# Eight down projections in seven products, six pairs of k's each, where six had four pairs

## The chip, the cores and the metric

The kernel runs on one core of one Trainium2 chip. The metric is the device time of one execution in microseconds (us). The kernel before took 2079.3 us (median of three runs, 2079.28 to 2080.11).

## The reference

Two layers over 256 tokens of width 2048, all in float32. The first layer mixes with a state space model and a gated recurrence, the second with windowed attention; after each comes the same MLP, whose up projection is 2048 to 8192 and whose down projection is 8192 to 2048. What the change touches is the down projection and what reads its result: the norm ahead of attention after the first MLP, and the output after the second.

```python
def squared_relu_mlp(xn, w_up, w_down):
    return jnp.square(jax.nn.relu(xn @ w_up)) @ w_down

def reference(...):
    h = x
    for layer in range(DEPTH):
        ...
        h = h + y.astype(h.dtype)
        h = h + squared_relu_mlp(rms_norm(h, mlp_norm[layer]), mlp_w_up[layer], mlp_w_down[layer])
    return h
```

## The kernel before

**Three matmuls for a product.** Each float32 operand is split into a high part in the matmul's own format and the rest (`hi`, `lo`), and a product is three matmuls: hi by hi, hi by lo, lo by hi. A weight is loaded as a unit of 1024 columns of 128 partitions (512 KB): `emit_dma` (L98) issues the load from SP into a buffer `raw`, `emit_split` (L131) lets ScalarE write `hi` (L141) and VectorE write `lo = raw - hi` (L142), and TensorE uses both (all matmuls are recorded at L190). `advance` (L145) hands the units out in one fixed order, a list called `units`. Loads go ahead through eight buffers: four of a pool (`raw`), and four more for odd units of an MLP (they are a part of the tile `chi`); a buffer takes its next load once the split of what it holds is done. Split weights have four buffers, and two more for every fourth unit.

**The MLP** (`mlp`, L984) works in four chunks c of 2048 hidden columns. `up(c)` makes the chunk's activations `ch[c]` (16 k's of 128 rows, 256 tokens in two halves t), `down(c)` multiplies them by 2048 rows of `w_down` and adds four blocks n of 512 columns to `h`. The plain way takes 8 products for a pair of k's, two halves t and two blocks n. `down_mixed` (L1038) takes 7 for the blocks 0 and 1, by sums and differences of the four quarters of an activation pair (`forms`, made in `up`, L1025 to L1032) and of the weights (`combine`, L117, on VectorE at L120). One pair j needs four units with names of their own: `t1` (two products), `t42` (two products, after two subtractions of 512 and 1024 columns that need t1's raw weights), later `b2` (two products) and `b12` (one product; its load is 256 KB, and its subtraction needs b2's raw weights). t1 has a subtraction of 512 columns, b12 too, b2 none. A product is accumulated in one of four banks `a_`, `c_`, `e_`, `f_`; after the last t42 ScalarE copies three of them, and after the last b12 VectorE forms the results (L1076 to L1081). The two blocks n = 2 and 3 stay plain: a plain unit is two k's by 512 columns and takes 12 matmuls of 512 columns, a unit t1, t42 or b2 takes 6, a b12 takes 3. `down_plan` (L310 to L321) is the order of the units of a chunk: four pairs (NS = 4) with plain units between them, then the pairs 4 to 7 of the blocks 0 and 1 as plain units. Below, a unit is named by kind and pair (t42.3), a plain one by block and pair (p3.1).

**The last chunk** (c = 3) is plain in all four blocks: `down` calls `xblock` for n = 0 to 3, adds each block to `h` and hands it to `nxt.block(n)`. That is `Norm.block` (L951) after the first MLP: squares on ScalarE, transposes on TensorE (L386) and two writes of the next operand `XT`; or `Out.block` (L964) after the second: two stores.

**The order.** A scheduler places the instructions on each engine's queue when the kernel is built, by the order of the program and its own idea of durations. Each engine then runs its queue in that order. So VectorE, standing at a combination whose load has not landed, does nothing else, though splits of older units are behind it.

Of the kernel before, what the change touches and what calls it, by code (L numbers as in the profile page):

```python
# [9 lines left out]
F32R = mybir.dt.float32r  # L10
# [7 lines left out]
P = 128  # L18
# [42 lines left out]
def hybrid_kernel(ctx: ExitStack, tc: tile.TileContext, x, even_norm, even_w_in, s5_lambda_re, s5_lambda_im,  # L61
# [208 lines left out]
    w_qkv, w_out1 = odd_w_qkv[0], odd_w_out[0]  # L270
    K16, K8 = list(range(16)), list(range(8))
    S5C, HC = 1024, 512
    in_cols = [0, 512]
# [13 lines left out]
    def add_mlp(l):  # L287
        def up(c):
            for n in range(8):
                add_units(mlp_w_up[l], K16, c * 2048 + n * 256, 256)  # L290

        def down(c):
            if c == 3:
                for n in range(4):
                    add_units(mlp_w_down[l], [c * 16 + k for k in K16], n * 512)
                return
            for kind, n, i in down_plan:
                if kind is None:
                    add_units(mlp_w_down[l], [c * 16 + 2 * i, c * 16 + 2 * i + 1], n * 512)
                else:  # L300
                    units.append((mlp_w_down[l], c * 16 + 2 * i + (kind in ("t42", "b2")),
                                  512 if kind == "b12" else 0, 2, kind))

        for c in range(4):
            up(c)
            down(c)
        ends.append(len(units))


    NS = 4  # L310
    plain = [(None, n, i) for n in (2, 3) for i in range(8)]
    down_plan = []
    for j in range(NS):
        down_plan += [("t1", 0, j), plain.pop(0), ("t42", 0, j), plain.pop(0)]
        if j < 2:
            down_plan.append(plain.pop(0))
    for j in range(NS):
        down_plan += [("b2", 0, j), plain.pop(0), ("b12", 0, j)]
        if plain and j < 2:
            down_plan.append(plain.pop(0))  # L320
    down_plan += plain + [(None, n, i) for n in (0, 1) for i in range(NS, 8)]  # L321

    add_mlp(0)
    qkv_cols = [2048, 0, 512, 1024, 1536]
    for c in qkv_cols:
        add_units(w_qkv, K16, c)
    out1_passes = [list(range(0, 8)), list(range(8, 12)), list(range(12, 16))]
# [616 lines left out]
    class Norm:  # L944
        def __init__(self, gain):
            self.gain, self.XT = gain, new_pair("x")
            self.ss = cp.tile([P, 2, 4], F32, name="ss" + gain)
            self.rs = cp.tile([P, 2], F32, name="rs" + gain)
            self.rs2 = cp.tile([P, 2], F32, name="rs2" + gain)

        def block(self, n):  # L951
            for t in range(2):
                j = t4([P, 512])
                S.activation(out=j, in_=h[:, t, n * 512:(n + 1) * 512], func=AF.Square,
                             accum_out=self.ss[:, t, n:n + 1])
            make_xT(h, self.XT, self.gain, 4 * n, 4)
            if n == 3:
                V.tensor_reduce(out=self.rs, in_=self.ss, axis=AX.X, op=ALU.add)
                V.tensor_scalar(out=self.rs, in0=self.rs, scalar1=1.0 / D, scalar2=EPS, op0=ALU.mult, op1=ALU.add)
                V.reciprocal(out=self.rs2, in_=self.rs)  # L960
                G.tensor_tensor(out=self.rs, in0=self.rs, in1=nhalf.to_broadcast([P, 2]), op=ALU.pow)
# [22 lines left out]
    def mlp(norm, nxt):  # L984
# [22 lines left out]
        def up(c):  # L1007
            ch[c] = new_pair("c")
            if c < 3:
                forms[c] = sp.tile([P, 2, NS, 4, P], F32R, tag="q1", name="forms", bufs=1)  # L1010
            for n in range(8):
# [11 lines left out]
                                op=ALU.subtract)  # L1023
                if c < 3 and n < NS:
                    a11, a21, a12, a22 = [r[:, k, t * P:(t + 1) * P] for k in range(2) for t in range(2)]  # L1025
                    s_ = t4([P, 4, P])
                    for o, a, b, op in ((0, a21, a22, ALU.add), (1, a11, s_[:, 0], ALU.subtract),
                                        (2, a11, a21, ALU.subtract), (3, a12, s_[:, 1], ALU.add)):
                        V.tensor_tensor(out=s_[:, o], in0=a, in1=b, op=op)
                    fh, fl = forms[c][:, 0, n], forms[c][:, 1, n]  # L1030
                    S.copy(out=fh, in_=s_)
# [6 lines left out]
        def down_mixed(c):  # L1038
# [15 lines left out]
            def form(j, i):  # L1054
                return F[:, 0, j, i], F[:, 1, j, i]

            for kind, n, j in down_plan:
# [15 lines left out]
                elif kind == "b12":  # L1073
                    triple(e_, *form(j, 2), *w[0], False, j == NS - 1)
                    if j == NS - 1:
                        V.tensor_tensor(out=v, in0=e_, in1=s1, op=ALU.add)  # L1076
                        hadd(0, 1, s1)
                        hadd(0, 1, s6)
                        hadd(1, 0, v)
                        hadd(1, 1, v)  # L1080
                        hadd(1, 1, s5)  # L1081
                else:
                    if n not in accs:
# [14 lines left out]
        def down(c):  # L1098
            nonlocal nxt
            if c < 3:  # L1100
                return down_mixed(c)
            nxt = nxt()
            for n in range(4):
                acc = xblock(ch[c], K16, n == 3 and nxt.__class__ is Out)
                for t in range(2):
                    hadd(t, n, acc[t])
                nxt.block(n)

# [149 lines left out]

    acc = xblock(n1.XT, K16)
    kn = t4([P, 2, 4, 2, 64])  # L1260
# [12 lines left out]
    for g in range(4):  # L1273
        acc = xblock(n1.XT, K16)
        if g >= 2:
# [41 lines left out]
```

## Time and profile before

| | |
|---|---|
| median of three runs | 2079.3 us |
| the profiled execution's own time | 2076.72 us |
| its span, first to last instruction | 2074.9 us |
| TensorE busy | 2062.2 us (99%), 12144 matmuls, clock 1.0 throughout |
| VectorE busy | 1476.6 us (71%) |
| ScalarE busy | 1137.5 us (55%) |
| loads and stores | 397.75 MB, mean 192 GB/s |

Durations below are from that one execution. A matmul's busy time is longer than the distance from one start to the next, since matmuls are pipelined; what a matmul costs is read from a row of many back to back. DVE is VectorE, ACT ScalarE, PE TensorE, PEld its weight loads, SP the queue that issues the loads.

### The profile page before, as it was taken

The page shows a single profiled execution, that of the slowest core. Times are in us where ns is not written, and L with a number is a line of the kernel's source. Part 1 is how long each engine was busy: PE and PEld are TensorE (multiplying, and loading weights), DVE is VectorE, ACT ScalarE, POOL GpSimd, SP SyncE. Part 2 cuts the span into 40 slices and gives each one's busy share as a digit, 9 for nine tenths or more (in the row PEclk, how much of TensorE's full clock was granted, in tenths as well). Part 3 has the DMA queues.
Part 4 walks back from the last instruction along what each step waited for, and adds up shares of the span by engine and source line. Part 5 has one row for each costly group of instructions (what it writes and reads, how often), then busy time and mean ns, then how long its engine had stood idle before and what let it go on. Part 6 is the DMA issues. An engine that isn't in the chain of part 4 may idle for free. (4 is left out here: it accounts for less than half of the span.)

```text
span 2074.9 us, 31132 instructions
## 1 busy us (share of the span) xinstructions
PE 2062.2 (99%) x12144; PEld 1755.4 (85%) x12144; DVE 1476.6 (71%) x2100; ACT 1137.5 (55%) x1541; POOL 38.8 (2%) x38
## 2 busy tenths in 40 slices
PE   9999999999999999999999999999999999999999
PEld 8988988888888878888888888788888888888887
DVE  6799967777767767776655688777767776776653
ACT  5887554565545545554554477565545545554542
POOL 2000000000000000000000110000000000000000
PEclk9999999999999999999999999999999999999999
DMA  8444557565676586576554643556676576567552
GB/s 250 122 150 145 169 165 245 173 199 193 204 244 191 192 254 190 196 250 197 192 184 125 190 150 125 183 182 203 204 249 188 192 260 192 187 210 247 188 200 89
DMA packets 264739, 397.75 MB, mean 192 GB/s; under 512 B 14888, under 2 KB 148560, under 8 KB 264272
## 3 DMA queue, kind: packets, MB, share of 16 engines
q1 hardware_dynamic: 263168, 392.50, 59.7%
q8 instruction: 95, 1.56, 0.3%
q0 software_dynamic: 672, 2.15, 0.3%
q10 hardware_dynamic: 752, 1.12, 0.2%
q14 instruction: 52, 0.43, 0.1%
HBM read 393.62 MB, written 2.10 MB: 191 GB/s over the span
## 5 line engine op out<-in xcount | busy, mean ns | idle before, releaser
L141 ACT CAST whi<-raw 128x1024 fp32r<-128x1024 f32 (+1 forms) x479 | 494.1, 1034 | 524.8 <-PE acc L190 427.5
L142 DVE TENSOR_TENSOR wlo<-raw,whi 128x1024 fp32r<-128x1024 f32 (+1 forms) x479 | 571.0, 1200 | 243.5 <-ACT whi L141 242.7
L190 PE MATMUL acc<-x,whi 128*128 128x512 f32 (+1 forms) x2336 | 636.0, 359 | 0.0
L190 PEld LDWEIGHTS acc<-x,wlo 128*128 128x128 f32 x1952 | 367.7, 189 | 70.2 <-DVE wlo L142 0.3
L190 PE MATMUL acc<-x,wlo 128*128 128x256 f32 x1952 | 417.9, 279 | 0.1
L190 PEld LDWEIGHTS acc<-x,whi 128*128 128x128 f32 x2336 | 359.6, 190 | 1.5 <-issue 0.4
L190 PE MATMUL acc<-wlo,chi 128*128 128x512 f32 x664 | 260.1, 392 | 2.6 <-DVE wlo L142 2.4
L190 PE MATMUL acc<-whi,chi 128*128 128x512 f32 x664 | 260.4, 392 | 0.0
L190 PE MATMUL acc<-whi,clo 128*128 128x512 f32 x664 | 259.4, 391 | 0.0
L142 DVE TENSOR_TENSOR wlo<-chi,whi 128x1024 fp32r<-128x1024 f32 x138 | 165.5, 1199 | 108.4 <-ACT whi L141 108.3
L141 ACT CAST whi<-chi 128x1024 fp32r<-128x1024 f32 x138 | 142.5, 1032 | 160.7 <-PE acc L190 123.7
L141 ACT CAST clo<-chi 128x1024 fp32r<-128x1024 f32 x136 | 143.0, 1053 | 137.6 <-PE acc L190 110.0
L142 DVE TENSOR_TENSOR clo<-chi,clo 128x1024 fp32r<-128x1024 f32 x136 | 166.1, 1223 | 58.1 <-ACT clo L141 57.0
L190 PE MATMUL acc<-whi,x 128*128 128x512 f32 x576 | 181.4, 393 | 0.0
L190 PE MATMUL acc<-x,clo 128*128 128x512 f32 x960 | 176.9, 337 | 0.0
L190 PEld LDWEIGHTS acc<-x,clo 128*128 128x128 f32 x960 | 150.2, 188 | 21.3
L190 PEld LDWEIGHTS acc<-wlo,chi 128*128 128x128 f32 x664 | 124.7, 188 | 31.7 <-DVE wlo L142 6.8
L190 PEld LDWEIGHTS acc<-whi,chi 128*128 128x128 f32 x664 | 124.7, 188 | 26.4 <-issue 0.8
L190 PEld LDWEIGHTS acc<-whi,clo 128*128 128x128 f32 x664 | 124.7, 188 | 25.3
L190 PEld LDWEIGHTS acc<-whi,x 128*128 128x128 f32 x576 | 107.4, 188 | 22.4 <-issue 0.4
L190 PE MATMUL acc<-clo,chi 128*128 128x512 f32 x400 | 123.1, 389 | 0.0
L120 DVE TENSOR_TENSOR raw<-raw 128x512 f32<-128x512 f32 (+1 forms) x72 | 59.4, 824 | 89.0 <-DMA raw<-in_mlp_w_down_dram 52.7
(260 smaller groups left out, 2399.6 us busy)
## 6 DMA issues: line engine op xcount, KB each, us to landing
chi<-in_mlp_w_down_dram SPq DMA_DIRECT2D x146, 512.0 KB, 3.8
raw<-in_mlp_w_up_dram SPq DMA_DIRECT2D x134, 512.0 KB, 3.8
raw<-in_mlp_w_down_dram SPq DMA_DIRECT2D x134, 512.0 KB, 4.6
chi<-in_mlp_w_up_dram SPq DMA_DIRECT2D x122, 512.0 KB, 3.8
raw<-in_even_w_in_dram SPq DMA_DIRECT2D x79, 512.0 KB, 3.9
raw<-in_odd_w_qkv_dram SPq DMA_DIRECT2D x40, 512.0 KB, 3.7
raw<-in_even_w_out_dram SPq DMA_DIRECT2D x32, 512.0 KB, 4.1
raw<-in_odd_w_out_dram SPq DMA_DIRECT2D x32, 512.0 KB, 3.8
```

The costliest lines, as they stand in the source:

```text
L120: V.tensor_tensor(out=o, in0=a, in1=b, op=ALU.subtract)
L141: S.copy(out=hi[:, ks], in_=raw[:, ks])
L142: V.tensor_tensor(out=lo[:, ks], in0=raw[:, ks], in1=hi[:, ks].bitcast(F32), op=ALU.subtract)
L190: PE.matmul(o, a, b, start=start, stop=stop, skip_group_check=True, **kw)
```

## The change

All four chunks of both MLPs use `down_mixed`, with six pairs (NS = 6) instead of four in three chunks. The order of a chunk is new: in the first half t1, plain, t42, plain for each pair; in the second half b2, plain, b12 for the pairs 0, 1, 3, 4 and b2, b12 for the pairs 2 and 5; then the pairs 6 and 7 of the blocks 0 and 1, plain. The forms of pairs 4 and 5 lie in the pool of temporaries (`t4`, six buffers), which they hold until the chunk's last b12. In the last chunk the plain blocks 2 and 3 are finished first; after the sums, three banks are added to `h` at once, `nxt.block(2)` and `nxt.block(3)` come there, and the blocks 0 and 1 take their last four k's by `xblock` and come last. `Norm` finishes after its fourth block, whichever that is, and attention's projections take their k's in the order 8 to 15, 0 to 7.

```diff
--- before.py
+++ after.py
@@ -269,6 +269,8 @@
     w_in, w_glu, w_out0 = even_w_in[0], s5_w_glu[0], even_w_out[0]
     w_qkv, w_out1 = odd_w_qkv[0], odd_w_out[0]
     K16, K8 = list(range(16)), list(range(8))
+
+    K_LATE = list(range(8, 16)) + list(range(8))
     S5C, HC = 1024, 512
     in_cols = [0, 512]
     for hh in range(2):
@@ -290,10 +292,6 @@
                 add_units(mlp_w_up[l], K16, c * 2048 + n * 256, 256)
 
         def down(c):
-            if c == 3:
-                for n in range(4):
-                    add_units(mlp_w_down[l], [c * 16 + k for k in K16], n * 512)
-                return
             for kind, n, i in down_plan:
                 if kind is None:
                     add_units(mlp_w_down[l], [c * 16 + 2 * i, c * 16 + 2 * i + 1], n * 512)
@@ -307,23 +305,19 @@
         ends.append(len(units))
 
 
-    NS = 4
+    NS = 6
     plain = [(None, n, i) for n in (2, 3) for i in range(8)]
     down_plan = []
     for j in range(NS):
         down_plan += [("t1", 0, j), plain.pop(0), ("t42", 0, j), plain.pop(0)]
-        if j < 2:
-            down_plan.append(plain.pop(0))
     for j in range(NS):
-        down_plan += [("b2", 0, j), plain.pop(0), ("b12", 0, j)]
-        if plain and j < 2:
-            down_plan.append(plain.pop(0))
+        down_plan += [("b2", 0, j)] + ([plain.pop(0)] if j % 3 < 2 else []) + [("b12", 0, j)]
     down_plan += plain + [(None, n, i) for n in (0, 1) for i in range(NS, 8)]
 
     add_mlp(0)
     qkv_cols = [2048, 0, 512, 1024, 1536]
     for c in qkv_cols:
-        add_units(w_qkv, K16, c)
+        add_units(w_qkv, K_LATE, c)
     out1_passes = [list(range(0, 8)), list(range(8, 12)), list(range(12, 16))]
     for kts in out1_passes:
         for n in range(4):
@@ -944,6 +938,7 @@
     class Norm:
         def __init__(self, gain):
             self.gain, self.XT = gain, new_pair("x")
+            self.done = 0
             self.ss = cp.tile([P, 2, 4], F32, name="ss" + gain)
             self.rs = cp.tile([P, 2], F32, name="rs" + gain)
             self.rs2 = cp.tile([P, 2], F32, name="rs2" + gain)
@@ -954,7 +949,8 @@
                 S.activation(out=j, in_=h[:, t, n * 512:(n + 1) * 512], func=AF.Square,
                              accum_out=self.ss[:, t, n:n + 1])
             make_xT(h, self.XT, self.gain, 4 * n, 4)
-            if n == 3:
+            self.done += 1
+            if self.done == 4:
                 V.tensor_reduce(out=self.rs, in_=self.ss, axis=AX.X, op=ALU.add)
                 V.tensor_scalar(out=self.rs, in0=self.rs, scalar1=1.0 / D, scalar2=EPS, op0=ALU.mult, op1=ALU.add)
                 V.reciprocal(out=self.rs2, in_=self.rs)
@@ -1006,8 +1002,8 @@
 
         def up(c):
             ch[c] = new_pair("c")
-            if c < 3:
-                forms[c] = sp.tile([P, 2, NS, 4, P], F32R, tag="q1", name="forms", bufs=1)
+            forms[c] = sp.tile([P, 2, 4, 4, P], F32R, tag="q1", name="forms", bufs=1)
+            forms[c] = [forms[c][:, :, j] for j in range(4)]
             for n in range(8):
                 acc = ublock(XT, K16)
                 drain()
@@ -1021,13 +1017,15 @@
                 S.copy(out=ch[c].hi[:, ks, :], in_=r)
                 V.tensor_tensor(out=ch[c].lo[:, ks, :], in0=r, in1=ch[c].hi[:, ks, :].bitcast(F32),
                                 op=ALU.subtract)
-                if c < 3 and n < NS:
+                if n < NS:
                     a11, a21, a12, a22 = [r[:, k, t * P:(t + 1) * P] for k in range(2) for t in range(2)]
                     s_ = t4([P, 4, P])
                     for o, a, b, op in ((0, a21, a22, ALU.add), (1, a11, s_[:, 0], ALU.subtract),
                                         (2, a11, a21, ALU.subtract), (3, a12, s_[:, 1], ALU.add)):
                         V.tensor_tensor(out=s_[:, o], in0=a, in1=b, op=op)
-                    fh, fl = forms[c][:, 0, n], forms[c][:, 1, n]
+                    if n >= 4:
+                        forms[c].append(t4([P, 2, 4, P], F32R))
+                    fh, fl = forms[c][n][:, 0], forms[c][n][:, 1]
                     S.copy(out=fh, in_=s_)
                     V.tensor_tensor(out=fl, in0=s_, in1=fh.bitcast(F32), op=ALU.subtract)
 
@@ -1052,7 +1050,7 @@
                 return X.hi[:, k, t * P:(t + 1) * P], X.lo[:, k, t * P:(t + 1) * P]
 
             def form(j, i):
-                return F[:, 0, j, i], F[:, 1, j, i]
+                return F[j][:, 0, i], F[j][:, 1, i]
 
             for kind, n, j in down_plan:
                 hi, lo = advance()
@@ -1079,6 +1077,12 @@
                         hadd(1, 0, v)
                         hadd(1, 1, v)
                         hadd(1, 1, s5)
+                        if c == 3:
+                            for t, n, o in ((0, 0, a_), (1, 0, f_), (0, 1, c_)):
+                                hadd(t, n, o)
+                            nxt.block(2)
+                            nxt.block(3)
+                            break
                 else:
                     if n not in accs:
                         if n > 1:
@@ -1097,14 +1101,15 @@
 
         def down(c):
             nonlocal nxt
-            if c < 3:
-                return down_mixed(c)
-            nxt = nxt()
-            for n in range(4):
-                acc = xblock(ch[c], K16, n == 3 and nxt.__class__ is Out)
-                for t in range(2):
-                    hadd(t, n, acc[t])
-                nxt.block(n)
+            if c == 3:
+                nxt = nxt()
+            down_mixed(c)
+            if c == 3:
+                for n in range(2):
+                    acc = xblock(ch[c], list(range(2 * NS, 16)), n == 1 and nxt.__class__ is Out)
+                    for t in range(2):
+                        hadd(t, n, acc[t])
+                    nxt.block(n)
 
         for c in range(4):
             up(c)
@@ -1256,7 +1261,7 @@
             yield from step(None)
             yield 1.5
 
-    acc = xblock(n1.XT, K16)
+    acc = xblock(n1.XT, K_LATE)
     kn = t4([P, 2, 4, 2, 64])
     head_norm(acc, 4, kn, 2)
     for t in range(2):
@@ -1271,7 +1276,7 @@
                                in1=ka[0:64, :, ts_].bitcast(F32), op0=ALU.mult, op1=ALU.subtract)
     ag = []
     for g in range(4):
-        acc = xblock(n1.XT, K16)
+        acc = xblock(n1.XT, K_LATE)
         if g >= 2:
             drain(ag[g - 2])
         qn = t4([P, 2, 8, 1, 64])
```

Two places of the queues, as the build gives them. The first is VectorE in the second half of the first MLP's first chunk. `L120` is a combination, `L142` a split (128x512 is that of a b12), `L1036` or `L1034` an addition to `h`; the numbered names are buffers. Before, from the combination of b12.1 to that of b12.2 and on:

```order
L120 TENSOR_TENSOR raw_5798<-raw_5763,raw_5798 128x512
L142 TENSOR_TENSOR clo_4783<-chi_4782,clo_4783 128x1024
L1036 TENSOR_TENSOR h_4035<-t4_5579,h_4035 128x512
L142 TENSOR_TENSOR wlo_5807<-chi_4782,whi_5806 128x1024
L142 TENSOR_TENSOR wlo_5828<-raw_5738,whi_5827 128x512
L1036 TENSOR_TENSOR h_4035<-t4_5580,h_4035 128x512
L142 TENSOR_TENSOR wlo_5844<-raw_5763,whi_5843 128x1024
L120 TENSOR_TENSOR raw_5859<-raw_5824,raw_5859 128x512
```

Now, from the combination of b12.2 over those of b12.3 (the second L120) and b12.4 (the third):

```order
L120 TENSOR_TENSOR chi_4782<-raw_5896,chi_4782 128x512
L142 TENSOR_TENSOR wlo_5913<-raw_5836,whi_5912 128x512
L142 TENSOR_TENSOR clo_4783<-chi_4782,clo_4783 128x512
L1034 TENSOR_TENSOR h_4035<-t4_5596,h_4035 128x512
L120 TENSOR_TENSOR raw_5956<-raw_5928,raw_5956 128x512
L142 TENSOR_TENSOR wlo_5940<-chi_4782,whi_5939 128x1024
L142 TENSOR_TENSOR wlo_5959<-raw_5871,whi_5958 128x1024
L142 TENSOR_TENSOR wlo_5973<-raw_5896,whi_5972 128x1024
L120 TENSOR_TENSOR chi_4782<-chi_4782 128x512
```

Four splits stood between two combinations; now two small ones stand between the first two, three between the next. The loads follow the splits on SP's queue: the load of b12.3 goes into the buffer that the split of b12.0 sets free (the row behind the first L120), that of b2.4 into the one of b2.1 (the row behind the second L120), that of b12.5 into the one of b12.2 (two rows behind the third, after the split of p3.6).

The second place is TensorE at the end of the first MLP, where attention's first projection begins (its operand is `x`). Before:

```order
L190 MATMUL acc_10169<-wlo_10219,chi_8945 128x512
L190 MATMUL acc_10169<-whi_10218,clo_8946 128x512
L190 MATMUL acc_10345<-whi_10236,x_9683 128x512
L190 MATMUL acc_10345<-wlo_10237,x_9683 128x512
L190 MATMUL acc_10345<-whi_10236,x_9683 128x512 x2
```

Now:

```order
L190 MATMUL acc_10512<-wlo_10392,chi_9059 128x512
L190 MATMUL acc_10512<-whi_10391,clo_9060 128x512
L380 MATMUL m_10442<-cf_74,h_4035 128x128 x4
L380 MATMUL m_10494<-cf_74,h_4035 128x128 x4
L190 MATMUL acc_10588<-whi_10454,x_9845 128x512
L190 MATMUL acc_10588<-wlo_10455,x_9845 128x512
```

The projection followed the down projection at once; now eight transposes of the norm (L380, L386 before), which need additions to `h`, stand between them.

## The prediction

> **What bounds the kernel now.** I read the page's busy times, then the chain that ended last, then the waits, then VectorE's and TensorE's rows in one mixed down projection.
>
> ```profile
> PE 2062.2 (99%) x12144; PEld 1755.4 (85%) x12144; DVE 1476.6 (71%) x2100; ACT 1137.5 (55%) x1541; POOL 38.8 (2%) x38
> ```
> ```profile
> 1871.95 22.44 PE m L190 x99
> ...
> 2048.84 21.77 PE m L190 x96
> ```
>
> TensorE runs without a pause. The second fence, from the chain, gives a matmul's price: 22.44 / 99 and 21.77 / 96 are both 0.227 us. Removed matmuls are worth that much each, as long as TensorE stays the bound. The next rows (stretches of a mixed down projection, an `up` and the plain last chunk; per engine busy us and count, then clock, DMA share and GB/s) say who could take its place.
>
> ```profile
> 510.70:596.40 85.70, 85.04 (x375) 69.64 (x374) 60.66 (x66) 43.01 (x46) 0.00 (x0) 1.00 0.72 237
> 612.00:684.00 72.00, 72.00 (x415) 62.81 (x414) 53.98 (x72) 40.25 (x49) 0.00 (x0) 1.00 0.60 186
> 1034.50:1125.60 91.10, 91.10 (x416) 75.64 (x416) 48.01 (x54) 42.24 (x58) 0.95 (x1) 1.00 0.47 151
> ```
>
> VectorE (third pair of numbers) is busiest in the mixed chunk, 60.66 of 85.70 us, and there it also stands still, by the list of waits (total us, count, mean):
>
> ```profile
> DVE raw L120 <- DMA raw<-in_mlp_w_down_dram: 52.7, 30, 3.2
> DVE raw L120 <- issue: 35.6, 12, 3.8
> ...
> DVE chi L120 <- issue: 17.1, 6, 3.3
> ...
> PEld acc L190 <- DVE wlo L142: 7.1, 13, 1.8
> ...
> PE acc L190 <- DVE wlo L142: 2.4, 3, 1.3
> ```
>
> The first three rows are combinations that wait for their load: 105.4 us over six mixed chunks, 17.6 each. The last two are the little that reaches TensorE: 2.4 to 7.1 us in the whole kernel. So there is a second loop close under TensorE. A split frees a buffer, the next load is issued, its landing releases a combination, and only behind that stands the next split. Its pieces, on VectorE and then on TensorE:
>
> ```profile
> 540.51 2.35 DVE L142 TENSOR_TENSOR wlo<-raw,whi 128x1024 fp32r<-128x1024 f32 x2
> ...
> 546.72 0.69 DVE L120 TENSOR_TENSOR raw<-raw 128x512 f32<-128x512 f32 x1 [2.66 <-DMA raw<-in_mlp_w_down_dram]
> 547.33 1.22 DVE L142 TENSOR_TENSOR clo<-chi,clo 128x1024 fp32r<-128x1024 f32 x1
> 548.46 0.69 DVE L1036 TENSOR_TENSOR h<-t,h 128x512 f32<-128x512 f32 x1
> 549.07 1.22 DVE L142 TENSOR_TENSOR wlo<-chi,whi 128x1024 fp32r<-128x1024 f32 x1
> 550.20 0.69 DVE L142 TENSOR_TENSOR wlo<-raw,whi 128x512 fp32r<-128x512 f32 x1
> 550.80 0.69 DVE L1036 TENSOR_TENSOR h<-t,h 128x512 f32<-128x512 f32 x1
> 551.41 1.22 DVE L142 TENSOR_TENSOR wlo<-raw,whi 128x1024 fp32r<-128x1024 f32 x1
> 555.74 0.69 DVE L120 TENSOR_TENSOR raw<-raw 128x512 f32<-128x512 f32 x1 [3.11 <-issue]
> 556.35 1.22 DVE L142 TENSOR_TENSOR clo<-chi,clo 128x1024 fp32r<-128x1024 f32 x1
> 557.48 1.22 DVE L142 TENSOR_TENSOR wlo<-chi,whi 128x1024 fp32r<-128x1024 f32 x1
> ```
> ```profile
> 544.74 0.39 PE L190 MATMUL m<-whi,chi 128*128 128x512 f32 x1
> ...
> 557.74 0.39 PE L190 MATMUL acc<-whi,chi 128*128 128x512 f32 x1
> 558.76 0.50 PE L190 MATMUL acc<-wlo,chi 128*128 128x512 f32 x1 [0.63 <-DVE wlo L142]
> ```
>
> From start to start a combination or half split costs VectorE 0.61 us and a full split 1.13. The first of the two splits at 540.51 (t42.3) ends at 541.73, and TensorE begins that unit at 544.74: VectorE leads by 3.0 us. The split of p3.4 ends at 557.48 + 1.22 = 558.70, or 16.97 later. TensorE has 57 to 58 matmuls between, 13.0 us. VectorE falls back by 4.0 on a lead of 3.0, and TensorE should lose 1.0: its starts at 557.74 and 558.76 lie 1.02 apart. The same sum can be made for the new order.
>
> **The change, part by part.** *Matmuls.* A pair of k's costs 21 mixed (6 + 6 + 6 + 3) and 24 plain. There are 4 x 6 pairs in an MLP instead of 3 x 4; 12 x 3 x 2 = 72 matmuls go, 72 x 0.2267 = **-16.3 us**.
>
> *Forms* are made for twice as many pairs, in `up`, by rows (busy, mean ns):
>
> ```profile
> L1032 DVE TENSOR_TENSOR forms<-t,forms 128x512 fp32r<-128x512 f32 x24 | 16.4, 685 | 0.0
> L1029 DVE TENSOR_TENSOR t<-t,t 128x128 f32<-128x128 f32 x48 | 13.8, 288 | 0.8
> ```
>
> That is 4 x 0.288 + 0.685 = 1.84 us for a pair, at most six in an `up`, where VectorE has 72.00 - 53.98 = 18 us free and two pairs (3.7 us) come new, six (11 us) in the last chunk. I cost it at nothing; TensorE covers it.
>
> *More splits and combinations.* A new mixed pair adds four combinations (3 x 0.61 + 1.13) and one and a half splits (1.7): 4.7 us of VectorE, so 60.7 + 9.4 = 70 of some 83 us in a chunk that had four pairs. That fits as a sum; with the 17.6 us of waiting it doesn't fit, unless waits shrink.
>
> *The waits of the new order.* In the second half of a chunk, four splits used to stand between a combination and the next, the one that frees the buffer early among them. Now two, three or none do, as the order above shows. How long a load takes to land is read from single ones (the DMA view of the moments 541.7, 533.7, 526.0, then 506.9 and 548.5, when no packets were moving):
>
> ```profile
> raw<-in_mlp_w_down_dram SPq DMA_DIRECT2D x1, 256.0 KB, 4.8
> ...
> raw<-in_mlp_w_down_dram SPq DMA_DIRECT2D x1, 256.0 KB, 3.8
> ...
> raw<-in_mlp_w_down_dram SPq DMA_DIRECT2D x1, 512.0 KB, 5.3
> ...
> raw<-in_mlp_w_down_dram SPq DMA_DIRECT2D x1, 512.0 KB, 3.1
> ...
> chi<-in_mlp_w_down_dram SPq DMA_DIRECT2D x1, 512.0 KB, 3.5
> ```
>
> The bounds are 3.1 and 5.3 us. I take 4.5 and 4.8 for loads issued among others, 3.5 and, as no row shows a 256 KB load alone, 3.3 for those that will be alone; 0.1 from a split's end to the issue. The Trainium skill ("DMA: Bandwidth & Descriptors", section "Anatomy of one DMA — SWDGE (gpsimd) path") gives about 2.0 us fixed plus the bytes at 436 GB/s, fitted on another queue: an estimate of 2.6 us for 256 KB and 3.2 for 512 KB. The lone 512 KB at 3.1 us agrees, the 256 KB at 3.8 and 4.8 do not; by the skill's figures the stall worked out next would vanish and the time be about 2061.
>
> From the combination of b12.1:
> (a) 0.61, three splits (3.5 with the issue), the load of b12.2 at 4.5, 0.1: the combination of b12.2 at 8.7.
> (b) 0.61, the half split of b12.0 (0.69), a lone load at 3.3 and 0.1: b12.3 at 13.4.
> (c) 0.61, the split of b2.1 (1.22), a lone load at 3.5 and 0.1: b12.4, which needs b2.4, at 18.8.
> (d) 0.61, a split 1.13, the half split 0.69, the load at 4.8 and 0.1: b12.5 at 26.1.
> (e) 0.61, a half split 0.61, then the split of b2.4, 1.22: done at 28.6.
>
> The split that opens this stretch (t42.5) ends at 1.83, so VectorE takes 26.7 us. TensorE has 90 to 91 matmuls in it, 20.5 us. VectorE loses **6.2 us** per chunk.
>
> How much lead has it? At a mixed chunk's start:
>
> ```profile
> 505.74 1.22 DVE L142 TENSOR_TENSOR wlo<-raw,whi 128x1024 fp32r<-128x1024 f32 x1
> ...
> 514.82 0.39 PE L190 MATMUL m<-whi,chi 128*128 128x512 f32 x1
> ```
>
> t42.0's split ends at 506.96, used at 514.82: 7.9 us. In the first half of the new order a round has 36 matmuls (8.16 us) and on VectorE a load, two combinations and three splits of about 8.8 to 9.0 us; five rounds take 3.0 to 4.3. That leaves 3.6 to 4.9, where the trace of before shows 3.0 at the same point. I take 3.2. The stall is 6.2 - 3.2 = **3.0 us** a chunk, eight chunks alike: **+24.0**.
>
> *Waits of before* in those chunks go with their order: 2.4 (TensorE's row) to 7.1 (that of its weight loads); I take **-3**.
>
> *The end of the first MLP.* Attention's projection used to start from a finished operand. Now eight transposes stand ahead of it which need additions to `h` (0.69) behind at most two splits: 0 to 3 us, **+1**. At the kernel's end the last two blocks and their stores come as before: nothing.
>
> Sum: -16.3 + 24.0 - 3 + 1 = **+5.7**, from 2076.7 to 2082.4 us of the profiled execution. That execution lies 2.6 below the median of 2079.3, so **2085.0**. The stall decides: at S us a chunk the change is 8 S - 18.3, which is zero at S = 2.3.
>
> **The rivals.** *Loads land as if alone, and TensorE stays the bound.* With 3.2 us for every 256 KB load (a), (b) and (d) shrink by 1.3, 0.1 and 1.6: VectorE loses 3.2 on a lead of 3.2 and S is 0: -18.3, **2061.0**. For it: 3.1 and 3.5 were seen, and waiting VectorE means fewer loads in flight. Against: the chunk already draws 237 GB/s, and its 256 KB loads took 3.8 and 4.8. The Trainium skill ("Perfetto Trace Analysis", section "Identifying the Most-Contended Engine") says to optimise the engine with the highest occupancy first; by that rule, TensorE at 99% would give the 72 matmuls in full. Chance 0.33.
>
> *The first half keeps more lead.* With 4.0 us left, inside the 3.6 to 4.9 above, S is 2.2: 17.6 - 18.3, **2078.6**. The 3.0 of before had three plain units more in the first half, and other pairs. Chance 0.25.
>
> *No load lands like a lone one.* If (b) takes 4.7 and (c) 4.6, like loads in company, VectorE loses 6.2 + 2.5 = 8.7 and S is 5.5: +44 - 18.3, **2105**. It is slower from S = 2.3 on. For it speaks that five loads of a round draw on the same queue; against it that a waiting VectorE frees no buffers, so that the next load has no company. Chance 0.13.
>
> **How the numbers follow.** The forecast itself has 0.29. A measurement of this kernel tells about 0.2% from no change, 4.2 us; the forecast at +5.7 lies a little beyond. Faster 0.33 is the first rival, same 0.25 the second, slower 0.42 the forecast and the third. The forecast's own range is 2083 (S = 2.75) to 2092 (lead 3.0, and 5.0 for the loads of (a) and (d): S = 3.9). The low end of the whole takes the first rival with the old waits at 4.75, midway between their two rows, 2059; the high end is short of the third rival by one us, 2104, since a part of its 0.13 lies above.
>
> **What would show it.** Right: 12072 matmuls; waits of TensorE or its weight loads for VectorE's `wlo` (L142) rising from 2.4 and 7.1 to some 20 us, once in each mixed chunk's second half, near b2.4; combinations (L120) waiting for DMA at least twice the 105 us. Wrong: those TensorE waits stay under 8 us (first rival); the lead at t42.5 is over 4 us; TensorE's gaps lie in the first half or at the end of the first MLP instead, or exceed 4 us in a chunk.

## The result and the profile after

The changed kernel took **2107.8 us** (median of four runs, 2100.11 to 2112.09), the kernel before 2079.44 beside it: a ratio of 1.0137 (95% interval 1.0119 to 1.0155), 28 us slower. The forecast was 2085.0, slower by 5.7, in a range up to 2104. The sign was right, the size was not.

| | before | after |
|---|---|---|
| median | 2079.44 us | 2107.8 us |
| the profiled execution's own time | 2076.72 us | 2100.11 us |
| its span | 2074.9 us | 2098.0 us |
| matmuls | 12144 | 12072 |
| VectorE busy | 1476.6 us | 1627.1 us |
| waits of TensorE in the mixed chunks* | 4.8 us | 40.5 us |

*Worked out from the starts of the matmuls of 512 columns: each distance beyond 0.227 us, where it is longer by over 0.1, without a stretch at half clock (last section).

The page's busy times:

```profile
PE 2057.7 (98%) x12072; PEld 1739.5 (83%) x12072; DVE 1627.1 (78%) x2382; ACT 1191.2 (57%) x1619; POOL 38.8 (2%) x38
```

The 72 matmuls are gone. The chain that ended last was TensorE's alone before, and was followed back over a tenth of the span only. Now it reaches back over six tenths and runs through loads and VectorE:

```profile
PE 43%; DMA 10%; DVE 8%; issue 2%; ACT 0%; DVEq 0%; ACTq 0%
```

The waits (total us, count, mean), to be read beside those of before:

```profile
DVE raw L120 <- DMA raw<-in_mlp_w_down_dram: 120.8, 89, 3.2
...
DVE chi L120 <- DMA chi<-in_mlp_w_down_dram: 63.8, 27, 4.0
...
PEld m L190 <- DVE wlo L142: 42.4, 41, 2.9
PE m L190 <- DVE wlo L142: 26.5, 23, 2.4
```

Combinations waited 105 us in six chunks, now 185 in eight. TensorE's waits sit on `m`, the four banks of the sums, where t1, t42, b2 and b12 accumulate: forty-one, about five in each chunk, where the forecast had one. TensorE in the first and in the second half of the first mixed chunk:

```profile
544.62 0.39 PE L190 MATMUL m<-whi,chi 128*128 128x512 f32 x1
545.75 0.50 PE L190 MATMUL m<-wlo,chi 128*128 128x512 f32 x1 [0.74 <-DVE wlo L142]
...
566.78 0.39 PE L190 MATMUL m<-whi,chi 128*128 128x512 f32 x1
569.31 0.50 PE L190 MATMUL m<-wlo,chi 128*128 128x512 f32 x1 [2.15 <-DVE wlo L142]
```

The second pair is the second half's stall, at b2.1; the forecast looked for it near b2.4. The first pair is not in the forecast: TensorE stands at t1.4, in the first half. By chunk, TensorE lost 2.1, 2.4, 0.0, 1.7, 2.6, 2.2, 1.6 and 2.4 us in first halves, **15.0**, and 4.4, 3.3, 2.7, 3.3, 4.1, 3.0, 3.5 and 2.7 in second halves, **27.0**; of the 4.1 in the fifth chunk 1.5 are matmuls at half clock, so the waits of second halves are **25.5**. They sit mostly at b2.1, 19 us of them. VectorE ahead of b2.1, in the first chunk:

```profile
563.28 0.69 DVE L120 TENSOR_TENSOR chi<-raw,chi 128x512 f32<-128x512 f32 x1 [3.51 <-DMA chi<-in_mlp_w_down_dram]
...
567.43 0.69 DVE L120 TENSOR_TENSOR raw<-raw 128x512 f32<-128x512 f32 x1 [1.65 <-DMA raw<-in_mlp_w_down_dram]
568.04 1.22 DVE L142 TENSOR_TENSOR wlo<-chi,whi 128x1024 fp32r<-128x1024 f32 x1
```

The last row is the split of b2.1, behind the combinations of b12.2 and b12.3 and their waits. VectorE in the first half:

```profile
534.96 2.36 DVE L142 TENSOR_TENSOR wlo<-raw,whi 128x1024 fp32r<-128x1024 f32 x2
537.23 1.22 DVE L142 TENSOR_TENSOR clo<-chi,clo 128x1024 fp32r<-128x1024 f32 x1
540.11 0.69 DVE L120 TENSOR_TENSOR raw<-raw 128x512 f32<-128x512 f32 x1 [1.66 <-DMA raw<-in_mlp_w_down_dram]
540.71 1.22 DVE L142 TENSOR_TENSOR wlo<-chi,whi 128x1024 fp32r<-128x1024 f32 x1
542.61 1.95 DVE L120 TENSOR_TENSOR raw<-raw 128x512 f32<-128x512 f32 x2 [0.68 <-DMA raw<-in_mlp_w_down_dram]
544.48 2.35 DVE L142 TENSOR_TENSOR wlo<-raw,whi 128x1024 fp32r<-128x1024 f32 x2
```

and the landing times of the two loads issued at 536.2 and 537.3, when the splits of the first row set their buffers free:

```profile
raw<-in_mlp_w_down_dram SPq DMA_DIRECT2D x1, 512.0 KB, 3.8
...
raw<-in_mlp_w_down_dram SPq DMA_DIRECT2D x1, 512.0 KB, 5.2
```

The first row holds the splits of t1.3 and t42.3, the last those of t1.4 and t42.4. The combinations between them belong to t1.5 and t42.5, one pair ahead: their splits come 12 us later, but their loads have only just been issued. So the split of t1.4, whose weights landed at 529.5, waits until t42.5 has landed at 542.5 and been combined. It is done at 544.48 + 1.22 = 545.70, and TensorE, which wanted it at 544.85, goes on at 545.75.

The profiled execution accounts for itself: -16.3 for 72 matmuls, +40.5 - 4.8 for the waits, and +1.7 for a stretch at half clock (last section) make +21.1; it was 23.4 slower, and the other 2.3 are not accounted for. In the three other runs the mean granted clock was 0.996, 0.995 and 0.994 where the profiled one had 0.999, and the spans 7.5 to 12 us longer; 0.3% to 0.5% of the span is 6 to 10 us. By the mean clock, the median adds these.

### The profile page after: what moved, and what is told of

The parts are those of the page before. It is cut to its first block, busy times and chain, and to the rows that moved or that the text cites. A ratio compares the mean times of both kernels' runs of the same rounds, so it can differ in the third digit from the quotient of the medians.

```text
span 2098.0 us, 31493 instructions
## 1 busy us (share of the span) xinstructions
PE 2057.7 (98%) x12072; PEld 1739.5 (83%) x12072; DVE 1627.1 (78%) x2382; ACT 1191.2 (57%) x1619; POOL 38.8 (2%) x38
## 4 chain that ended last, share of the span: by engine, by line
PE 43%; DMA 10%; DVE 8%; issue 2%; ACT 0%; DVEq 0%; ACTq 0%
PE acc L190 36%; PE m L190 6%; DMA raw<-in_mlp_w_down_dram 6%; DVE wlo L142 5%; DMA chi<-in_mlp_w_down_dram 4%; DVE clo L142 1%; DVE raw L120 1%; PE m L1215 1%; PE m L380 0%; DMA chi<-in_mlp_w_up_dram 0%; PE m L1249 0%; DVE h L1034 0%; ACT whi L141 0%; ACT clo L141 0%; DVE chi L120 0%
## 5 line engine op out<-in xcount | busy, mean ns | idle before, releaser
L142 DVE TENSOR_TENSOR wlo<-raw,whi 128x1024 fp32r<-128x1024 f32 (+1 forms) x503 | 599.1, 1200 | 162.3 <-ACT whi L141 161.4
L141 ACT CAST clo<-chi 128x1024 fp32r<-128x1024 f32 (+1 forms) x148 | 148.7, 1006 | 159.2 <-PE acc L190 128.1
L120 DVE TENSOR_TENSOR raw<-raw 128x512 f32<-128x512 f32 (+1 forms) x160 | 136.1, 851 | 122.2 <-DMA raw<-in_mlp_w_down_dram 120.8
L190 PE MATMUL acc<-wlo,chi 128*128 128x512 f32 x528 | 207.5, 393 | 1.5 <-DVE wlo L142 1.5
L190 PE MATMUL acc<-whi,chi 128*128 128x512 f32 x528 | 207.5, 393 | 0.0
L142 DVE TENSOR_TENSOR wlo<-chi,whi 128x1024 fp32r<-128x1024 f32 (+1 forms) x150 | 174.3, 1162 | 42.5 <-ACT whi L141 42.4
L190 PE MATMUL acc<-whi,clo 128*128 128x512 f32 x528 | 206.6, 392 | 0.0
L141 ACT CAST whi<-chi 128x1024 fp32r<-128x1024 f32 (+1 forms) x150 | 150.6, 1004 | 97.1 <-PE acc L190 70.1
L142 DVE TENSOR_TENSOR clo<-chi,clo 128x1024 fp32r<-128x1024 f32 (+1 forms) x148 | 171.8, 1162 | 13.1 <-ACT clo L141 10.7
L190 PE MATMUL acc<-clo,chi 128*128 128x512 f32 x528 | 164.3, 389 | 0.0
L190 PEld LDWEIGHTS acc<-wlo,chi 128*128 128x128 f32 x528 | 99.3, 188 | 26.1 <-DVE wlo L142 6.2
L190 PE MATMUL m<-wlo,chi 128*128 128x512 f32 x224 | 91.3, 407 | 26.1 <-DVE wlo L142 25.8
```

Of the source, the lines that this page charges most:

```text
L120: V.tensor_tensor(out=o, in0=a, in1=b, op=ALU.subtract)
L141: S.copy(out=hi[:, ks], in_=raw[:, ks])
L142: V.tensor_tensor(out=lo[:, ks], in0=raw[:, ks], in1=hi[:, ks].bitcast(F32), op=ALU.subtract)
L190: PE.matmul(o, a, b, start=start, stop=stop, skip_group_check=True, **kw)
```

## The experiments

My **theory** after the result: VectorE runs its queue in order and stands at combinations whose loads were issued late; TensorE runs out of splits because of where combinations stand in that queue. **Rival one**: VectorE's work, 70 of 83 us in a chunk, is too much. **Rival two**: the loss lies at the chunks' ends, the new end of the MLP or the clock. Line numbers in these kernels are up to three off where an edit adds lines.

### No combinations

```diff
-        if kind is not None:
-            combine(kind, raw)
```

> Leaves out all combinations (L120), so VectorE has neither their 136 us of work nor their 186 us of waits for loads; the blocks 0 and 1 of the down projections are therefore not the product. Theory (VectorE's queue stands at combinations whose load lands late, and TensorE runs out of splits): TensorE's waits at L190 go from 42 us to under 5 and the time is 2060 us, within 5. Rival one (VectorE's added work is too much for a chunk): the same, 2060. Rival two (the loss lies at the chunks' ends, in the changed end of the MLP or in the granted clock whatever VectorE does): 2090 or more.

2056.73 us, ratio 0.9887 (0.9873 to 0.9902), as the theory and rival one had it. No wait of TensorE for VectorE is left in the mixed chunks. Rival two falls: chunk ends, the norm's place and attention's k's are as in the changed kernel, and the time is 51 us lower.

### The same work without the wait

```diff
-            V.tensor_tensor(out=o, in0=a, in1=b, op=ALU.subtract)
+            o = dead["h"][:, 0, 0:w]
+            V.tensor_tensor(out=o, in0=o, in1=dead["z"].to_broadcast([P, w]), op=ALU.subtract)
```

> Every combination is replaced by a subtraction of zero from h of the same 512 or 1024 columns on VectorE: the same work, but nothing in it waits for a load (the blocks 0 and 1 are again not the product). Theory: the work alone fits, 70 of 83 us in a chunk, so TensorE's waits stay under 8 us and the time is 2060 to 2067 us. Rival one (the work is too much): over 2090 us, with TensorE's waits over 30 us. Rival two: 2090 or more.

2071.47 us, ratio 0.9958 (0.9942 to 0.9973), above the theory's range, far below rival one's. The mixed chunks have no wait of TensorE for a split. VectorE did the subtractions, in 157.1 us with nothing to wait for:

```profile
L123 DVE TENSOR_TENSOR h<-h,z 128x512 f32<-128x512 f32 (+1 forms) x192 | 157.1, 818 | 0.6
```

What it lost lies elsewhere: at the first `up` of each MLP the starts of TensorE's matmuls have gaps of 0.3, 3.1, 1.7 and 0.3 us, and its weight loads there wait for ScalarE's `clo`. VectorE does such subtractions there, among the last activations: since nothing holds them back, they were queued early. Behind these gaps TensorE runs at half clock for 3.41 us each time, another 1.7. Two times 7.1 us are some 14, so the chunks themselves stand near 2057. Work alone is not the bound.

### The same combinations later in the queue

The block under `issue_after` is queued on VectorE behind a given instruction, here the split of the unit ahead:

```diff
-            combine(kind, raw)
+            with tc.issue_after(los[i - 1]):
+                combine(kind, raw)
...
-            V.tensor_tensor(out=lo[:, ks], in0=raw[:, ks], in1=hi[:, ks].bitcast(F32), op=ALU.subtract)
+            los[i] = V.tensor_tensor(out=lo[:, ks], in0=raw[:, ks], in1=hi[:, ks].bitcast(F32), op=ALU.subtract).ins
```

> All combinations are kept, but each is queued on VectorE behind the split of the unit just ahead of it, so up to four splits later than now; loads and everything else as they are. Theory: a load has landed some 10 us before its unit's split, so most of the 186 us of waiting at combinations goes and the time falls to 2060 to 2075 us; what could remain is VectorE waiting for ScalarE between a combination and its own split, some 1 us each time nothing stands between. Rival one: 2095 to 2110, since the work is the same. Rival two: 2095 to 2110.

2055.35 us, ratio 0.9884 (0.9867 to 0.99), 5 us below the theory's range. The work is the same, 80% busy VectorE included, and the time is 52 us below the changed kernel's and 25 below before's. VectorE in a round of the first half:

```profile
528.44 2.43 DVE L143 TENSOR_TENSOR wlo<-raw,whi 128x1024 fp32r<-128x1024 f32 x2
531.78 1.23 DVE L143 TENSOR_TENSOR clo<-chi,clo 128x1024 fp32r<-128x1024 f32 x1 [0.91 <-ACT clo L142]
532.93 0.69 DVE L120 TENSOR_TENSOR raw<-raw 128x512 f32<-128x512 f32 x1
533.53 1.22 DVE L143 TENSOR_TENSOR wlo<-chi,whi 128x1024 fp32r<-128x1024 f32 x1
534.67 1.94 DVE L120 TENSOR_TENSOR raw<-raw 128x512 f32<-128x512 f32 x2
536.60 2.43 DVE L143 TENSOR_TENSOR wlo<-raw,whi 128x1024 fp32r<-128x1024 f32 x2
```

No combination waits for a load. A round takes 536.60 - 528.44 = 8.16 us, TensorE's own pace. Rival one falls here.

> As the kernel with combinations queued behind the split of the unit ahead, but behind that of the unit before it: one split remains between a combination and its own split, to cover ScalarE's cast. Theory: 2060 to 2072 us, within 6 us of the other late kernel and below it if the casts are what remains there. Rivals one and two: 2095 to 2110.

With `los[i - 2]` in the place of `los[i - 1]`: 2055.85 us, ratio 0.9885 (0.987 to 0.99), the same and again below the range. Nothing remained for the casts to explain.

### Which half: only t1 and t42 late, or only b12

```diff
-            with tc.issue_after(los[i - 1]):
+            with tc.issue_after(los[i - 1]) if kind in ("t1", "t42") else nullcontext():
```

> Only the combinations of the first half (t1, t42) are queued behind the split of the unit ahead; those of b12 stay where they were. Theory (the lead is lost in the first half, and the second half's loss of 6 us then falls on none): TensorE's waits of the first half, 15 us, go, VectorE enters the second half with 5 us or more of lead instead of 2.3, and the second half's 27 us fall under 8: 2058 to 2068 us. Rival (the second half alone makes its stall, the lead hardly matters): 15 us and a little of the clock go, 2088 to 2094.

2056.94 us, ratio 0.9891 (0.9872 to 0.9909), 1 us below the theory's range: the first half alone brings nearly everything. The combinations of b12 still wait, 62 us where they waited 90 in the changed kernel:

```profile
DVE chi L120 <- DMA chi<-in_mlp_w_down_dram: 60.3, 24, 4.7
DVE raw L120 <- DMA raw<-in_mlp_w_down_dram: 1.4, 4, 0.5
```

From the split of t42.5 to that of b2.4 VectorE takes 24.6 to 26.9 us, near the 26.7 of the forecast, and TensorE's matmuls 20.4. But the lead at t42.5 is 5.1 to 5.7 us in place of 1.9 to 2.8, and TensorE waits 0.4 us in all.

> Only the combinations of the second half (b12) are queued behind the split of the unit ahead; those of t1 and t42 stay. Theory: the first half still costs its 15 us and leaves no lead, the second half costs under 6 in place of 27: 2070 to 2080 us with the clock. Rival: 2060 to 2068, since the second half was the source.

With `("b12",)`: 2074.52 us, ratio 0.9969 (0.9954 to 0.9983), in the theory's range. The first halves cost 15.5 us as in the changed kernel, the second nothing: VectorE takes 22.85 us there. The expectation that no lead is left was wrong: it is 5.3 us at t42.5, since combinations of b12 had stood ahead of that split too.

### The kernel before with late combinations

> The kernel before, all combinations queued behind the split of the unit ahead. Theory: only its 4.8 us of TensorE's waits for VectorE can go: 3 to 6 us faster than before. Then the 72 matmuls are worth the rest, 16 to 20 us, between this kernel and the six pairs with late combinations. Rival (the late queue brings something beyond those waits): over 8 us faster than before.

2071.3 us, ratio 0.9958 (0.9943 to 0.9974): 8.5 us faster by the medians, 5 to 12 by the interval, 5.9 by the profiled executions. The theory had 3 to 6, the rival over 8, and the interval holds both; the old order's waits were worth more than the 3 us of the forecast. The six pairs with late combinations are 2071.3 - 2055.4 = 15.9 us below this kernel, where the forecast priced 72 matmuls at 16.3.

### Four pairs in all eight

Chunk order and NS as before, the rest as changed.

> The changed kernel with four pairs and the chunk order of before, in all eight down projections: the last chunks stay mixed, with the norm or the output behind the sums and attention's k's in the new order. 24 matmuls fewer than before, -5.4 us; two more mixed chunks at 0.8 us of waits, +1.6; the end of the MLP 0 to 2. Theory (the loss lies in the order for six pairs): 2 to 5 us faster than before. Rival (it lies in the mixed last chunk and its end): slower than before by 5 us or more.

2078.16 us (2074.25 to 2083.05 in ten runs), ratio 0.9995 (0.9981 to 1.0009): neither. It excludes rival two's 5 us, but it spreads over 9 us from run to run, too much to show the 2 to 5 us gain. Its profiled execution, one of the longer of the ten at 2081.71, has 13 us of waits in eight mixed chunks, where the expectation had 6.4. The same with late combinations:

> Four pairs in all eight down projections, the end of the MLP and attention's k's as in the changed kernel, all combinations queued behind the split of the unit ahead, so that no wait for VectorE blurs it. Against the kernel before with late combinations (2071.3 us) it has 24 matmuls less, -5.4 us. If the end of the first MLP costs the 1 us of the forecast: 2066 to 2068. If the mixed last chunk or its end costs more than it saves: 2071 or more. If it costs nothing: 2065 to 2066.

2066.12 us, ratio 0.9935 (0.9916 to 0.9954); 5.2 below the kernel before with late combinations, against 5.4 for 24 matmuls. The mixed last chunk and the end of the first MLP cost 0.2 to 0.3 us by these medians, not the forecast's 1; the two kernels did not run side by side.

### Doubled loads

```diff
-            nc.sync.dma_start(out=raw[:, 0:w // 512], ...
+            for _ in range(2 if kind == "t42" else 1):
+                nc.sync.dma_start(out=raw[:, 0:w // 512], ...
```

> The changed kernel, with the load of every t42 issued twice into its buffer, the second behind the landing of the first: the data is complete some 3 to 5 us later and SP's queue stands meanwhile. Theory (VectorE stands at the combination of t42 until it lands, with ready splits behind it): five rounds in eight chunks lose 2 to 4 us each, 2180 to 2270 us. Rival (the loss is VectorE's work, landing times matter little): under 2130.

> The same doubled loads of t42 in the kernel whose combinations are queued behind the split of the unit ahead. There a t42 lands 10 to 18 us before its split is done. Theory (the place in VectorE's queue decides, not the load itself): under 2066 us, 10 us or less above the same kernel with single loads. Rival (loads bound these chunks wherever the combinations stand): it loses as much as the changed kernel does by doubling, within a third.

The changed kernel goes to 2167.59 us, 60 us more: neither (the theory had 72 at least, the rival 22 at most). By the profiled executions it is 65 more, 42 of waits in the mixed chunks and 23 of matmuls at half clock there. With late combinations it is 2054.58, no more than with single loads (2055.35). The waits of the first:

```profile
DVE raw L121 <- DMA raw<-in_mlp_w_down_dram: 180.8, 88, 5.9
...
PEld acc L191 <- DVE wlo L143: 59.1, 32, 4.6
PE acc L191 <- DVE wlo L143: 45.8, 23, 4.2
PEld m L191 <- DVE wlo L143: 31.9, 28, 3.9
```

and of the second:

```profile
DVE raw L121 <- DMA raw<-in_mlp_w_down_dram: 29.8, 22, 3.1
PEld m L192 <- DVE wlo L144: 0.7, 2, 0.4
```

A load that lands later costs 60 us, the clock included, in one order of the queue and nothing in the other. This shows that the place in the queue decides, and not the loads by themselves.

### Combinations on GpSimd

```diff
-            V.tensor_tensor(out=o, in0=a, in1=b, op=ALU.subtract)
+            G.tensor_tensor(out=o, in0=a, in1=b, op=ALU.subtract)
```

> All combinations on GpSimd in place of VectorE; it does nothing else in these chunks. Theory: VectorE loses 158 us of work and all waits at loads; if GpSimd's subtraction of 512 columns is under some 2.5 us (no row shows it; 24 of 512 and 1024 columns in a chunk, 30 times that in 83 us and more), TensorE's waits stay under 10 us: 2055 to 2066 us. If it is slower, GpSimd becomes the bound and the time is above 2100.

2054.32 us, ratio 0.9873 (0.9853 to 0.9894), just below the theory's range and as good as the late queue (they did not run side by side, and 1 us is not told apart). Now GpSimd stands at the loads, and nobody else is behind it:

```profile
POOL raw L120 <- DMA raw<-in_mlp_w_down_dram: 292.1, 62, 82.4
POOL chi L120 <- DMA chi<-in_mlp_w_down_dram: 119.9, 30, 7.9
```

### Which of the two waits in the first half

> Only the combinations of t42 are queued behind the split of the unit ahead; those of t1 and b12 stay. Theory (t42's combinations, with the longest landings, 4.4 to 6.0 us, and 1.87 us of work, stand ahead of the split of the older t1, which TensorE needs 18 matmuls before t42): t1's lead in rounds 3 to 5 rises from about -0.5 to 1 us or more, TensorE's waits in the first half fall from 15 us to under 5, and the second half's 27 to under 15: 2057 to 2076 us. Rival (the wait at t1's load counts as much): half of the first half's waits stay and the second half is as now: 2085 to 2100.

> Only the combinations of t1 are queued behind the split of the unit ahead; those of t42 and b12 stay. With t42 alone the first half's waits had gone to 3.7 us, but VectorE still entered the second half with 2.0 us, because t1's combinations still waited. If both waits of a round cost alike: TensorE's waits between 15 and 35 us in all, 2068 to 2090 us. If t1's wait is what takes the lead: lead of 4 us or more at t42.5, waits under 10 us, 2056 to 2066 us. If t1's doesn't matter: as the changed kernel, 2095 to 2112.

| late | median, ratio (interval) | waits of TensorE, first, second halves | lead at t42.5 |
|---|---|---|---|
| none | 2107.8, 1.0137 (1.0119 to 1.0155) | 15.0, 25.5 us | 1.9 to 2.8 us |
| t1 | 2097.35, 1.0089 (1.0063 to 1.0114) | 15.2, 20.2 | 1.6 to 1.7 |
| t42 | 2078.49, 0.9991 (0.9979 to 1.0002) | 3.7, 20.3 | 1.9 to 2.5 |
| t1, t42 | 2056.94, 0.9891 (0.9872 to 0.9909) | 0.0, 0.4 | 5.1 to 5.7 |

The waits leave out matmuls at half clock, 4.5 us with only t1 late and 1.5 with none. The result for t42 lies between the ranges of its expectation; that for t1 lies in the range for "t1's doesn't matter". Moving t42's combination takes 11 of the 15 us of waits from the first halves, as the theory had it. But the second halves, where the theory expected under 15 us, keep 20, and the lead there comes back only when neither t1 nor t42 waits (or when b12's combinations are moved, above). By what landed when a wait ended, VectorE stood 72 us at t1's combinations and 24 at t42's in the changed kernel; with t42's moved it stands 75 at t1's, with t1's moved 75 at t42's. So t1's does matter once t42's is out of the way; the two do not add up, and there is no price for each alone.

## Why the forecast was wrong

**What held.** TensorE was the bound of before and 72 matmuls were worth 16 us: 15.9 where no wait blurs it. The loop from split over load and combination to the next split was the mechanism, and it did turn the gain around. The second half was sized rightly on VectorE, with some luck: it took 26.1 to 28.0 us from t42.5 to b2.4 (26.7 or 26.8 forecast), but pieces of it were off in opposite ways. In the first chunk the loads of b12.2, b12.3 and b12.5, issued at 558.1, 564.6 and 575.6, landed after 5.1, 2.7 and 5.6 us:

```profile
chi<-in_mlp_w_down_dram SPq DMA_DIRECT2D x1, 256.0 KB, 5.1
...
raw<-in_mlp_w_down_dram SPq DMA_DIRECT2D x1, 256.0 KB, 2.7
...
chi<-in_mlp_w_down_dram SPq DMA_DIRECT2D x1, 256.0 KB, 5.6
```

where 4.5, 3.3 and 4.8 were taken; in the other seven chunks b12.5's took 3.8 to 4.0. The place was another, too: TensorE waits mostly at b2.1 and not near b2.4. The forecast's own steps hold that: by (b), b2.1 is split 13.4 us behind t42.5, TensorE has 39 matmuls, 8.8 us, between, and with the lead of 2.3 that there was this makes 2.3 us a chunk, 18 in all, where 19 were measured. At b2.4 they would make 3.9 a chunk, 31, and the second halves lost 25.5; that difference stays open.

**The step that failed** is the lead in the first half: "five rounds take 3.0 to 4.3. That leaves 3.6 to 4.9 ... I take 3.2", with no wait of TensorE in the first half. Two things were wrong in it.

First, the round. From the split of one t1 to that of the next, VectorE takes 11.3, 11.1, 10.4 and 9.5 us on the mean of the eight chunks (7.9 in the fifth round), not 8.8 to 9.0. So the lead at t42, 9.2 us at t42.0 where 7.9 was taken, is down to 3.1 after three rounds. The rows above give the fourth: from the split of t1.3 (done at 536.18) to that of t1.4 (545.70) are 9.52 us: t42.3's split 1.14, the load of t42.5 with its issue 5.2, 0.1, the combination 1.87 and the split 1.22. The forecast's round leaves 4.5 to 4.7 for the landing; t42.5's took 5.1 on the mean, and t42.4's, in the third round, 6.0. In the first two rounds the loads took 4.4 and 4.7, but there VectorE still has the last activations of `up` to do, which the forecast's round did not contain, as in the second round of the first chunk:

```profile
514.96 0.68 DVE L1012 TENSOR_TENSOR t<-acc,t 128x512 f32<-128x512 f32 x1
...
516.70 0.68 DVE L1013 SCALAR_TENSOR_TENSOR t<-t,rst 128x512 f32<-128x512 f32 x1
...
523.00 0.68 DVE L1018 TENSOR_TENSOR clo<-t,chi 128x512 fp32r<-128x512 f32 x1
```

At 0.6 us each from start to start, these are 1.8 us of a round of 10.9.

Second, the unit at which the lead was read. In before's trace it was read at t42, the tighter of the two there (3.0 us at t42.2 on the mean, 6.9 at t1.2). In the new order the split of t1 stands right ahead of t42's, behind the combination of the t42 one pair ahead, and TensorE needs t1 18 matmuls, 4.1 us, before t42. Over the eight chunks the lead at t1.1 to t1.4 is 4.5, 1.6, -0.7 and -0.8 us on the mean while at t42.1 to t42.4 it is 6.8, 4.5, 3.1 and 3.0. So a lead of 3 at t42, safe in the forecast, is none at t1 (3.0 + 1.1 for t42's split - 4.1). The order of the queue would have shown it.

So TensorE loses 15.0 us in first halves, which the sum did not have, and the second halves, entered with 2.3 us and not 3.2, lose 25.5 in place of 24.0. With the lead of 5.4 that the late t1 and t42 give, the second half costs 0.4.

**The other terms.** Waits of before: 3 taken, 5.9 in the profiled executions; the row of the weight loads, 7.1, was the nearer bound. The end of the first MLP: 1 taken, 0.2 to 0.3 found with four pairs. The clock was not in the sum: +1.7 us in the profiled execution and 6 to 10 in the others.

**The rivals.** The third, heaviest one gave 2105, near the result, but by luck: lone loads did land faster (2.7 us for 256 KB), and what the forecast lacked came from the first half and the clock. The first and the second rival asked for a lead that was not there. The first rival's time, 2061.0, is reached, and passed, only when the wait is taken out of VectorE's queue: 2054 to 2057.

## What to carry to other kernels

On an engine that runs its queue in order, ask of each instruction that waits for a transfer what stands behind it and when its own result is needed: here combinations stood 12 us ahead of their use, and moving them a few splits back was worth 52 us with no work saved. Work out a lead for every unit in the order in which the consumer takes them, in every part of the round, since the tightest unit of the old order need not be that of the new. A loss per round counts as often as there are rounds, so the landing time in it deserves its upper bound, and its sum of work must hold what is left over from the stretch before.

The six pairs with late combinations (2055.4 us, ratio 0.9884, 0.9867 to 0.99), or with combinations on GpSimd (2054.3, ratio 0.9873, 0.9853 to 0.9894), beat both kernels.

## What the runs showed of the hardware

**Waits of about 2 us can cost the clock.** In the changed kernel TensorE stood from 1527.4 to 1530.0 us (2.25 us by the row), and its next matmuls start 0.43 us apart, then 0.227 again. By windows (the clock is the last figure but two):

```profile
1527.30:1530.00 2.70, 0.45 (x3) 0.03 (x2) 1.89 (x3) 1.15 (x2) 0.00 (x0) 1.00 0.21 79
1530.00:1533.40 3.40, 3.40 (x8) 2.75 (x9) 2.21 (x2) 0.86 (x1) 0.00 (x0) 0.50 0.57 173
1533.40:1538.00 4.60, 4.60 (x21) 3.77 (x21) 4.15 (x5) 1.44 (x4) 0.00 (x0) 1.00 0.82 270
```

3.4 us at half clock cost 1.7. Seven other gaps of 2.0 to 2.6 us beyond a matmul's own time kept the full clock in this execution. In the others the lower mean clock suggests that more were hit; no trace shows where. With only t1 late, three more stretches follow waits of 1.9 to 2.1 us at b2.1, and begin 1.0 to 1.4 us after TensorE goes on:

```profile
1529.60:1533.00 3.40, 3.40 (x10) 2.63 (x9) 1.99 (x3) 1.04 (x1) 0.00 (x0) 0.50 0.82 268
1707.10:1710.50 3.40, 3.40 (x9) 2.63 (x8) 1.93 (x4) 1.04 (x1) 0.00 (x0) 0.50 0.82 254
1884.60:1888.00 3.40, 3.40 (x9) 2.65 (x9) 1.84 (x3) 1.04 (x1) 0.00 (x0) 0.50 0.90 279
```

Each lasts 3.41 us by the record of the clock, as does the one above. The Trainium skill ("TensorE: Matmul & The Clock Gate", section "Part 1: The HAM clock gate (the "warmup" mystery)") puts the half clock after an idle window of about 3.4 us that runs freely. The length of the slow stretch and its chance nature agree; here a wait of 2.25 us was enough.

**GpSimd's subtractions lengthen VectorE's.** A subtraction of 512 columns takes 1.8 us on GpSimd and 0.69 on VectorE. With them on GpSimd, a full split on VectorE takes 1.43 us on the mean instead of 1.22. Of all 751 full splits, the 256 that overlap a subtraction on GpSimd take 1.96 us on the mean, the others 1.22:

```profile
L120 POOL TENSOR_TENSOR raw<-raw 128x512 f32<-128x512 f32 x112 | 202.3, 1809 | 793.0 <-DVE clo L1018 385.3 <-DMA raw<-in_mlp_w_down_dram 292.1 <-DVE t L1025 98.4
L120 POOL TENSOR_TENSOR raw<-raw 128x1024 f32<-128x1024 f32 x48 | 153.2, 3191 | 3.8
```
```profile
L142 DVE TENSOR_TENSOR wlo<-raw,whi 128x1024 fp32r<-128x1024 f32 x485 | 689.3, 1428 | 183.3 <-ACT whi L141 181.2
```
```profile
L142 DVE TENSOR_TENSOR wlo<-raw,whi 128x1024 fp32r<-128x1024 f32 x459 | 558.2, 1222 | 239.0 <-ACT whi L141 238.2
```

(the last row is before's). VectorE was busy 1701.3 us then, more than with the combinations on it, 1635.2, and the time did not suffer. The Trainium skill ("SBUF — State Buffer", section "SBUF: two separate sides") has an exclusive lock on a port pair that these two engines share, taken by a VectorE operation with two inputs from SBUF as well; the longer splits agree with that.
